# The dt chain ahead of the first gate's function, in a laid order, in a Mamba-2 and differential-attention trunk

## The chip, the core and the metric

The kernel runs on one core of a Trainium2 chip. That core has five engines with an instruction queue each: TensorE (PE in the profile), VectorE (DVE), ScalarE (ACT), GpSimd (POOL) and SyncE (SP), which issues most DMAs. An engine takes the instructions of its queue strictly in order and waits on semaphores for the others. The metric is the device time of one execution in microseconds, lower is better.

## The reference, cut to what matters

The input is a sequence of 512 tokens of 1024 features. Layer A is a Mamba-2 mixer, layer B a differential attention that uses one shared key and value projection of layer A's output.

```python
h = rms_norm(x, norm_g)
zxbcdt = h @ w_in                       # z: 2048, x: 2048, B: 1024, C: 1024, dt: 32
xbc = silu(causal_depthwise_conv(xbc, conv_w, conv_b))
dt = softplus(dt_raw + dt_bias)         # 32 heads
a = -exp(a_log)
y = ssd_chunked_scan(xs * dt, a * dt, bm, cm)
y = y + d_skip * xs
u = y * silu(z)                         # the gate
u = u * rsqrt(mean over 256 features of u*u + eps) * g
x = x + u @ w_out
k, v = shared_kv(x); x = x + diff_attention(x, k, v); return rms_norm(x)
```

The scan treats the 32 heads in eight groups (four heads each, one B and one C of 128 states per group).

## The kernel before, in words

Float32 products are made out of three matmuls each: a matrix is split into a rounded part `hi` and a rest `lo`, and hi·hi, hi·lo and lo·hi are summed in a PSUM bank. Weights arrive in 1 MB segments (two `raw` buffers); ScalarE writes `whi` in four casts per segment and VectorE `wlo` in four subtractions (two buffers each). Tokens are not normalised before the products of layer A: the reciprocal root mean square of each token is put on the results, as `r_col` (one value per token, for results with tokens on partitions) or `r_row` (the same as a row, for results with features on partitions).

The work around the change is the start of layer A:

- **The gate of the first two groups** (`pz0`, four PSUM banks for four times 128 tokens): segments 0 and 1. Before the change `z_out` evicts it on ScalarE, as SiLU of bank times `r_col`, eight instructions of 128x256 (`zs`).
- **The dt chain**: `scales` makes `r_col` from the squared sums of the tokens and, through a matmul of a diagonal (`aps_r`), `r_row`. 32 small matmuls make `ps_dt`; `pre`, `e1`, `q1`, `pl`, `dtp`, `adt` and a scan make the decays `acs`, which go to memory (`acs_d`) and come back spread over the partitions as `dec`, 1 MB per group. GpSimd subtracts and masks `dec`, ScalarE exponentiates it. `tok` is a transposed copy of dtp, acs and toe.
- **Group g** (`group_proj`): two segments into four banks `pg{g}_0..3` (B, C and two halves of x). `conv` works in place on a bank: VectorE multiplies by `r_row`, ScalarE writes `xc` (Identity with a weight and a bias), VectorE adds three shifted products, ScalarE takes SiLU of `xc`. The bank is free again after the last shifted product. Group 0's are xc16, xc24, xc0, xc1, in this order; group 1's are xc17, xc25, xc2, xc3.
- **The scan of group g** (`ssd`): `pbt`, `pcb`, `pxt{g}_0`, `pxt{g}_1` transpose or multiply the xc tiles (pxt0_0 reads xc0, pxt0_1 reads xc1), `xdt`, `dx`, `xe`, `psA`, `psB`, `pyd` follow, then the gating `dx*zs`, its squares, a root, the scaled `tmp` and its transposes `pyt`.

Four PSUM banks carry the tag `mm`: `pz0` holds all four, so `pg0_0` waits until the first of them is evicted, and group 1's banks wait for group 0's convolutions.

The order on each engine is made at build time by a list scheduler with its own idea of costs. The wrappers `V`, `A` and `T` pin instructions to the order in which they are written while their `on` is set. `fetch`, called from `use`, lays the casts of a segment two segments ahead of the products, at high priority. A ScalarE function that is not in the loaded table set costs an `ACT_TABLE_LOAD`; the loads stand in the built program.

Of the kernel before, what the change touches and what calls it, by code (L numbers as in the profile page):

```python
# [25 lines left out]
H = 32  # L26
# [12 lines left out]
C_GA, C_GK, C_GB, C_GG, C_SG, C_DTB, C_AL, C_CB, C_CW = 0, 8, 16, 24, 40, 41, 42, 43, 75  # L39
# [24 lines left out]
def trunk(ctx, tc, x, x_t, par, w_dt, w_in, w_out, w_kvqg, w_bo, d_skip, lam_qk, fin_g, out):  # L64
    nc = tc.nc
    V, A, T = (Ordered(tc, e) for e in (nc.vector, nc.scalar, nc.tensor))
    GP = nc.gpsimd

    const = ctx.enter_context(tc.tile_pool(name="const", bufs=1))
    res = ctx.enter_context(tc.tile_pool(name="res", bufs=1))  # L70
    wp = ctx.enter_context(tc.tile_pool(name="wp", bufs=2))
    small = ctx.enter_context(tc.tile_pool(name="small", bufs=2))
# [13 lines left out]
    def long_bank(name):  # L86
        return psum.tile([P, 512], F32, tag="long", name=name)
# [10 lines left out]
    prm = const.tile([P, C_CB], F32, name="prm")  # L98
# [3 lines left out]
    ident = const.tile([P, P], F32, name="ident")  # L102
# [18 lines left out]
    ready = {}  # L121
# [166 lines left out]
    def run(gen):  # L288
        for _ in gen:
            pass  # L290
# [18 lines left out]
            sq = small.tile([P, D], F32, tag="wide", name=f"sq{t}", bufs=2)  # L309
        A.activation(sq, x_tok[:, t, :], AF.Square, accum_out=ss[:, t:t + 1])  # L310

    def scales(tag, ss):

        V.tensor_scalar(out=ss, in0=ss, scalar1=ROOT2 / D, scalar2=ROOT2 * EPS, op0=ALU.mult, op1=ALU.add)
        col = const.tile([P, NT], F32, tag="r_col", name=f"{tag}r_col")
        V.tensor_copy(col, rsqrt(ss, NT, "y"))
        w = small.tile([P, NT + 1, P], F32, tag="wide", name=f"{tag}diag", bufs=2)
        GP.memset(w[:, NT], 1.0)
        for t in range(NT):
            GP.tensor_tensor(out=w[:, t], in0=ident, in1=col[:, t:t + 1].to_broadcast([P, P]), op=ALU.mult)  # L320
        ps = long_bank(f"{tag}ps_r")
        T.on = True
        T.matmul(ps, lhsT=w[:, NT], rhs=w[:, 0:NT].rearrange("p t n -> p (t n)"), start=True, stop=True)
        T.on = False
        row = res.tile([P, S], F32, tag="r_row", name=f"{tag}r_row")
        A.copy(row, ps)
        return col, row
# [18 lines left out]
    def tok_mm(ps, t, b, w):  # L346
        tk = slice(t * P, (t + 1) * P)
        for k in range(4):
            kk = 4 * b + k
            mm3(ps, (hh[:, kk, tk], hl[:, kk, tk]), (w[0][:, k, :], w[1][:, k, :]), b == 0 and k == 0, b == 1 and k == 3)  # L350
            yield
# [10 lines left out]
    zt = {}  # L362
# [22 lines left out]
    begin = small.tile([P, 1], F32, name="begin", bufs=1)  # L385
# [14 lines left out]
    for k in range(4, KD):  # L400
        split_x(k)
    fetch(2)
    for t in range(NT):
        nc.sync.dma_start(x_tok[:, t, :], x[t * P:(t + 1) * P, :])
    ss = sm.tile([P, NT], F32, name="ass")
    for t in range(NT):
        squares(ss, t)
    r_col, r_row = scales("a", ss)
    V.tensor_scalar(out=sg1, in0=prm[:, C_SG:C_SG + 1], scalar1=0.5 * (1.0 - LAM0), scalar2=None, op0=ALU.mult)
    dtw_raw = sm.tile([P, KD, H], F32, name="dtw_raw")  # L410
    nc.sync.dma_start(dtw_raw[:], w_dt)

    V.tensor_tensor(out=dtw_raw, in0=dtw_raw, in1=prm[:, C_GA:C_GA + KD].unsqueeze(2).to_broadcast([P, KD, H]), op=ALU.mult)
    ps_dt = ss_bank("ps_dt")
    T.on = True
    for k in range(KD):
        for c in range(NQ):  # L420
            T.matmul(ps_dt[c * H:(c + 1) * H, 0:P], lhsT=dtw_raw[:, k, :], rhs=xt[k // 2][:, k % 2, c * P:(c + 1) * P],
                     start=k == 0, stop=k == KD - 1)
    T.on = False
    pre = sm.tile([P, P], F32, name="pre")
    for c in range(NQ):
        sl = slice(c * H, (c + 1) * H)
# [2 lines left out]
    e1 = sm.tile([P, P], F32, name="e1")  # L429
    A.activation(e1, pre, AF.Abs)  # L430
    A.activation(e1, e1, AF.Exp, scale=-1.0)

    q1 = sm.tile([P, P], F32, name="q1")
    V.tensor_scalar(out=q1, in0=e1, scalar1=2.0, scalar2=None, op0=ALU.add)
# [8 lines left out]
    V.scalar_tensor_tensor(out=pl, in0=pl, scalar=2.0, in1=q1, op0=ALU.add, op1=ALU.mult)  # L443
    dtp = sm.tile([P, P], F32, name="dtp")
    V.scalar_tensor_tensor(out=dtp, in0=pre, scalar=0.0, in1=pl, op0=ALU.max, op1=ALU.add)
    ea = sm.tile([P, 1], F32, name="ea")
    A.activation(ea, prm[:, C_AL:C_AL + 1], AF.Exp)
    adt = sm.tile([P, P], F32, name="adt")
    V.tensor_scalar(out=adt, in0=dtp, scalar1=ea, scalar2=-1.0, op0=ALU.mult, op1=ALU.mult)
    ones = sm.tile([P, P], F32, name="ones")  # L450
# [3 lines left out]
    acs_d = tc.dram_tile([H, NQ, P], F32, name="acs_d")  # L454
    for c in range(NQ):
        nc.sync.dma_start(acs_d[:, c, :], acs[c * H:(c + 1) * H, :])
    toe = sm.tile([P, P], F32, name="toe")
    A.activation(toe, acs, AF.Exp, scale=-1.0, bias=acs[:, P - 1:P])
    dsk = const.tile([P, H], F32, name="dsk")
    nc.sync.dma_start(dsk[:], d_skip.partition_broadcast(P))  # L460


    w0 = use(("z", 0, 1))
    for t in range(NT):
        run(tok_mm(pz0[t], t, 1, w0))
        z_out(0, t, pz0[t])


    ps_tt = ss_bank("ps_tt")
    for i, src in enumerate((dtp, acs, toe)):  # L470
        T.transpose(ps_tt[:, i * P:(i + 1) * P], src, ident)
    tok = const.tile([P, 4, NQ, H], F32, name="tok")
    V.tensor_copy(tok[:, 0:3].rearrange("p a c h -> p (a c h)"), ps_tt[:, 0:3 * P])
    A.activation(tok[:, 3], tok[:, 1], AF.Exp)
    dt_tok, acs_tok, toe_tok, eacs_tok = (tok[:, i] for i in range(4))


    def z_proj(j):
        pz = [mm_bank(f"pz{j}_{t}") for t in range(NT)]
        for b in range(2):  # L480
            w = use(("z", j, b))
            for t in range(NT):
                yield from tok_mm(pz[t], t, b, w)
                if b:
                    z_out(j, t, pz[t])

    def conv(ps, ft, name, bufs):
        xc = bp2.tile([P, S], F32, tag=f"xc_{name}", name=f"xc{ft}", bufs=bufs)
        at = C_CW - C_CB + 4 * ft
        cw = [prc[:, at + k:at + k + 1] for k in range(4)]  # L490

        u = ps
        V.tensor_tensor(out=u, in0=ps, in1=r_row, op=ALU.mult)
        A.activation(xc, u, AF.Identity, scale=cw[3], bias=prc[:, ft:ft + 1])
        for k in (2, 1, 0):
            d = 3 - k
            V.scalar_tensor_tensor(out=xc[:, d:], in0=u[:, :S - d], scalar=cw[k], in1=xc[:, d:], op0=ALU.mult, op1=ALU.add)
        A.activation(xc, xc, AF.Silu)
        return xc

    def group_proj(g):
        pg = [mm_bank(f"pg{g}_{i}") for i in range(4)]
        fts = [(16 + g, "b", 1), (24 + g, "c", 2), (2 * g, "x0", 1), (2 * g + 1, "x1", 1)]
        outs = []
        for b in range(2):
            wh, wl = use(("g", g, b))
            for i in range(4):
                cs = slice(i * P, (i + 1) * P)
                for k in range(4):
                    kk = 4 * b + k  # L510
                    mm3(pg[i], (wh[:, k, cs], wl[:, k, cs]), (hh[:, kk, :], hl[:, kk, :]),
                        b == 0 and k == 0, b == 1 and k == 3)
                    yield
# [34 lines left out]
    def decays(gs):  # L548

        for g in gs:  # L550
            hs = slice(R * g, R * g + R)
            both = bp.tile([P, N_DEC], F32, tag="dec", name=f"dec{g}", bufs=2)
            dec = both[:, 0:R * NQ * P].rearrange("p (h c l) -> p h c l", h=R, c=NQ)
            een = both[:, R * NQ * P:].rearrange("p (h q) -> p h q", h=R)
            nc.sync.dma_start(both[:, 0:R * NQ * P],
                                acs_d[hs].rearrange("h c l -> (h c l)").partition_broadcast(P))
            GP.tensor_copy(een, dec[:, :, 1:3, P - 1])
            for h in range(R):
                GP.tensor_tensor(out=dec[:, h], in0=dec[:, h], in1=acs_tok[:, :, R * g + h].unsqueeze(2).to_broadcast([P, NQ, P]), op=ALU.subtract)
                GP.affine_select(out=dec[:, h], in_=dec[:, h], compare_op=ALU.is_ge, fill=-BIG, base=0,  # L560
                                 pattern=[[0, NQ], [1, P]], channel_multiplier=-1)
            decs[g] = (dec, een, both)

        for g in gs:
            A.activation(decs[g][2], decs[g][2], AF.Exp)

    def ssd(g):
        bc, cc, x0, x1 = conv_out.pop(g)
# [516 lines left out]
    y, f, o, dst = half(3, 0)  # L1085
# [77 lines left out]
```

## Time and profile before

| | us |
|---|---|
| median of three runs | 709.59 (709.17 to 709.61) |
| the profiled execution's own time | 709.26 |
| its span, first to last instruction | 707.5 |
| PE busy | 697.5 (99%) |
| DVE, ACT, POOL busy | 519.5, 430.1, 111.7 |
| granted TensorE clock | 0.999 |

Busy time of PE says that it nearly always had work; where it had none is read from its waits and from the starts of its matmuls, which in a full stream of 128x512 follow each other at 0.227 us although each row is shown with 0.39 us.

### The profile page before, as it was taken

How to read it: one execution, taken by the hardware profiler on the slowest of the kernel's cores; microseconds unless marked ns; L12 is line 12 of the kernel's file. 1: busy time of each engine (PE TensorE's matmuls, PEld its weight loads, DVE VectorE, ACT ScalarE, POOL GpSimd, SP SyncE). 2: the span in 40 equal slices, each digit the busy share in tenths (PEclk: the TensorE clock that was granted, in tenths of full speed). 3: DMA queues.
4: the chain of work that ended last, by engine and by line, in shares of the span. 5: the costliest groups of instructions: out<-in, count | busy, mean ns of one | idle time of the engine just before them, and what ended most of it. 6: DMA issues, size and time to landing. Idle time of an engine off the chain costs nothing.

```text
span 707.5 us, 10916 instructions
## 1 busy us (share of the span) xinstructions
PE 697.5 (99%) x4030; PEld 590.8 (84%) x4030; DVE 519.5 (73%) x1197; ACT 430.1 (61%) x955; POOL 111.7 (16%) x158
## 2 busy tenths in 40 slices
PE   9999999999999999999999999999999999999996
PEld 7777888888888888888888879888988998899885
DVE  5479964889579569568997856566767757785886
ACT  6739672764744537538535367676667766756556
POOL 0009421503306024050110101000000000000002
PEclk9999999999999999999999999999999999999999
DMA  8644313333133331331221311412211221122003
GB/s 303 246 151 152 120 59 127 113 120 120 60 119 120 120 120 60 119 120 59 73 100 68 120 60 36 152 60 93 87 61 60 75 105 59 61 101 80 31 0 120
DMA packets 13493, 70.88 MB, mean 100 GB/s; under 512 B 1792, under 2 KB 3328, under 8 KB 6016
## 3 DMA queue, kind: packets, MB, share of 16 engines
q1 hardware_dynamic: 13008, 69.90, 27.6%
q8 instruction: 32, 0.52, 0.3%
q10 hardware_dynamic: 432, 0.28, 0.1%
q14 instruction: 21, 0.17, 0.1%
HBM read 68.02 MB, written 2.16 MB: 99 GB/s over the span
## 4 chain that ended last, share of the span: by engine, by line
PE 88%; ACT 4%; DVE 3%; DMA 3%; issue 1%; SPq 0%; ACTq 0%; DVEq 0%
PE pg L55 20%; PE po L55 16%; PE pz L55 9%; PE pt L55 7%; PE pv L55 6%; PE pq L55 6%; PE pk L55 6%; PE pb L55 3%; DMA raw<-in_w_in 3%; PE sc L55 3%; PE pyd L55 2%; PE pc L55 2%; ACT whi L55 1%; PE pxt L55 1%; PE psA L55 1%; PE pyt L55 1%
## 5 line engine op out<-in xcount | busy, mean ns | idle before, releaser
L55 DVE SCALAR_TENSOR_TENSOR wlo<-raw,prm,whi 128x512 fp32r<-128x512 f32 (+1 forms) x256 | 150.8, 637 | 56.1 <-ACT whi L55 55.6
L55 ACT ACTIVATE whi<-raw,prm 128x512 fp32r<-128x512 f32 (+1 forms) x256 | 136.8, 607 | 62.8 <-issue 13.1
L55 PE MATMUL pg<-a_hi,whi 128*128 128x512 f32 x256 | 102.2, 399 | 0.4 <-ACT zs L55 0.3
L55 PE MATMUL pg<-a_lo,whi 128*128 128x512 f32 x256 | 101.1, 395 | 0.0
L55 PE MATMUL pg<-a_hi,wlo 128*128 128x512 f32 x256 | 100.0, 396 | 0.0
L55 DVE SCALAR_TENSOR_TENSOR xc<-pg,prc,xc 128x511 f32<-128x511 f32 (+2 forms) x96 | 69.9, 739 | 7.5 <-ACT xc L55 7.1
L55 PEld LDWEIGHTS pg<-a_hi,whi 128*128 128x128 f32 x256 | 48.1, 188 | 10.5 <-ACT zs L55 0.6
L55 PEld LDWEIGHTS pg<-a_hi,wlo 128*128 128x128 f32 x256 | 48.1, 188 | 9.8
L55 PEld LDWEIGHTS pg<-a_lo,whi 128*128 128x128 f32 x256 | 48.1, 188 | 9.6
L55 PE MATMUL po<-whi,yh 128*128 128x512 f32 x128 | 50.8, 397 | 0.4 <-ACT yh L55 0.4
L55 PE MATMUL po<-wlo,yh 128*128 128x512 f32 x128 | 50.8, 397 | 0.0
L55 PE MATMUL po<-whi,yl 128*128 128x512 f32 x128 | 50.1, 395 | 0.0
L55 PE MATMUL pz<-wlo,a_hi 128*128 128x512 f32 x128 | 49.3, 394 | 0.0
L55 PE MATMUL pz<-whi,a_hi 128*128 128x512 f32 x128 | 48.9, 396 | 0.0
L55 PE MATMUL pz<-whi,a_lo 128*128 128x512 f32 x128 | 48.8, 390 | 0.0
L968 POOL TENSOR_TENSOR ot<-x_tok,fg 128x512 f32<-128x512 f32 x4 | 5.0, 1290 | 246.4 <-DVE x_tok L55 246.4
L55 ACT ACTIVATE s<-s,mx 128x128 f32<-128x128 f32 (+3 forms) x64 | 35.5, 556 | 9.7 <-DVE mx L55 9.3
L55 ACT ACTIVATE xc<-pg,prc 128x512 f32<-128x512 f32 x32 | 24.8, 776 | 24.5 <-DVE pg L55 19.6
L595 POOL TENSOR_TENSOR xe<-xdt,tok 128x256 f32<-128x256 f32 x24 | 14.1, 614 | 161.5 <-DVE xdt L55 161.5
L55 DVE CUSTOM_DVE_ANT_0 s<-sc,bias 128x128 f32<-128x128 f32 (+3 forms) x64 | 29.3, 487 | 12.3 <-PE sc L55 11.8
L55 PE MATMUL pv<-whi,b_hi 128*128 128x256 f32 x128 | 36.9, 289 | 0.0
L55 PE MATMUL pv<-whi,b_lo 128*128 128x256 f32 x128 | 36.2, 283 | 0.0
(238 smaller groups left out, 1676.5 us busy)
## 6 DMA issues: line engine op xcount, KB each, us to landing
raw<-in_w_in SPq DMA_DIRECT2D x22, 1024.0 KB, 4.9
raw<-in_w_kvqg SPq DMA_DIRECT2D x16, 1024.0 KB, 4.8
dec<-acs_d SPq DMA_DIRECT2D x8, 1024.0 KB, 4.8
raw<-in_w_out SPq DMA_DIRECT2D x8, 1024.0 KB, 4.7
raw<-in_w_bo SPq DMA_DIRECT2D x4, 1024.0 KB, 4.7
x_tok<-in_x SPq DMA_DIRECT2D x4, 512.0 KB, 9.0
out<-ot SPq DMA_DIRECT2D x6, 256.0 KB, 2.3
raw<-in_w_in SPq DMA_DIRECT2D x4, 256.0 KB, 4.7
```

What stands on the lines that cost most here:

```text
L55: i = op(*args, **kw)
L595: GP.tensor_tensor(out=xe[:, c], in0=xdt[:, c], in1=toe_tok[:, c, hs].unsqueeze(2).to_broadcast([P, R, HD]), op=ALU.mult)
L968: GP.tensor_tensor(out=o, in0=y, in1=f, op=ALU.mult)
```

## The change

- The gate's eight SiLUs on the banks become eight `tensor_scalar` on VectorE (`z_raw`: bank times `r_col`), three banks' worth right behind `r_col`, the fourth behind the copy of `r_row`. SiLU is then taken in place on `zs` by ScalarE, queued behind the last convolution function of group 0 (`issue_after(conv_end)`).
- The gate's second half of products stands ahead of the dt chain in the program, and the casts of segments 2 and 3 are laid by hand: segment 2 behind the first three banks, segment 3 behind the scan. VectorE and ScalarE are pinned over the whole chain.
- A one-element `Exp` is put behind the copy of `r_row`; `ea` moves behind the first Exp of the chain; `tok[:, 3]` (an Exp) moves to where the decays are exponentiated.
- The loads of `dtw_raw` and `dsk` are written ahead of segments 2 and 3.

```diff
+    w0 = ready.pop(("z", 0, 1))
     for t in range(NT):
         nc.sync.dma_start(x_tok[:, t, :], x[t * P:(t + 1) * P, :])
+    dtw_raw = sm.tile([P, KD, H], F32, name="dtw_raw")
+    nc.sync.dma_start(dtw_raw[:], w_dt)
+    nc.sync.dma_start(dsk[:], d_skip.partition_broadcast(P))
+    splits = {n: load(n) for n in (2, 3)}
...
-    r_col, r_row = scales("a", ss)
+    for t in range(NT):
+        run(tok_mm(pz0[t], t, 1, w0))
+    V.on = True
+    r_col, diag = scale_cols(ss)
+
+    def z_raw(t):
+        for i in range(2):
+            zt[i, t] = bp2.tile([P, 256], F32, tag="zs", name=f"zs0_{t}_{i}", bufs=12)
+            V.tensor_scalar(out=zt[i, t], in0=pz0[t][:, i * 256:(i + 1) * 256], scalar1=r_col[:, t:t + 1], scalar2=None, op0=ALU.mult)
+
+    for t in range(3):
+        z_raw(t)
+    A.on = True
+    for piece in splits[2]():
+        lay(piece)
...
+    A.copy(r_row, ps_r)
+    A.activation(begin, ident[:, 0:1], AF.Exp)
+    z_raw(3)
...
+    A.activation(ea, prm[:, C_AL:C_AL + 1], AF.Exp)
...
         nc.sync.dma_start(acs_d[:, c, :], acs[c * H:(c + 1) * H, :])
+    for piece in splits[3]():
+        lay(piece)
     A.activation(toe, acs, AF.Exp, scale=-1.0, bias=acs[:, P - 1:P])
-    w0 = use(("z", 0, 1))
-    for t in range(NT):
-        run(tok_mm(pz0[t], t, 1, w0))
-        z_out(0, t, pz0[t])
+    A.on = V.on = False
...
-        A.activation(xc, xc, AF.Silu)
+        conv_end[0] = A.activation(xc, xc, AF.Silu)
...
+        if g == 0:
+            with tc.issue_after(conv_end[0].ins):
+                for t in range(NT):
+                    for i in range(2):
+                        A.activation(zt[i, t], zt[i, t], AF.Silu)
...
+        if gs[0] == 0:
+            A.activation(tok[:, 3], tok[:, 1], AF.Exp)
```

What the scheduler makes of it on ScalarE, from the load ahead of group 0's first SiLU to its last, before the change (numbers behind the names tell buffers apart; xc16, xc24, xc0 and xc1 are group 0's tiles, whi5 is segment 5, dec0 and dec1 are the decays of groups 0 and 1):

```order
L55 ACT_TABLE_LOAD
L55 ACTIVATE xc16_570<-xc16_570 128x512
L55 ACTIVATE xc0_608<-pg0_2_484,prc_72 128x512
L55 ACTIVATE whi5_548<-raw5_546,prm_70 128x512 x4
L55 ACTIVATE xc24_589<-xc24_589 128x512
L55 ACTIVATE xc1_627<-pg0_3_485,prc_72 128x512
L55 ACT_TABLE_LOAD
L55 ACTIVATE dec0_442<-dec0_442 128x2056
L55 COPY bt0_662<-pbt0_658 128x384
L55 ACT_TABLE_LOAD
L55 ACTIVATE xc0_608<-xc0_608 128x512
L55 ACTIVATE xc1_627<-xc1_627 128x512
```

The same stretch with the change, from segment 5 on (ahead of these rows stand the Identities of xc16, xc24 and xc0, a table load and the SiLU of xc16; behind them the eight SiLUs of `zs`):

```order
L55 ACTIVATE whi5_549<-raw5_547,prm_70 128x512 x4
L55 ACT_TABLE_LOAD
L55 ACTIVATE dec0_442<-dec0_442 128x2056
L55 ACTIVATE xc1_628<-pg0_3_486,prc_72 128x512
L55 ACT_TABLE_LOAD
L55 ACTIVATE xc24_590<-xc24_590 128x512
L55 COPY bt0_671<-pbt0_667 128x384
L55 ACTIVATE xc0_609<-xc0_609 128x512
L55 ACT_TABLE_LOAD
L55 ACTIVATE dec1_461<-dec1_461 128x2056
L55 ACT_TABLE_LOAD
L55 ACTIVATE xc1_628<-xc1_628 128x512
```

The SiLU of xc24 and the Identity of xc1 stand behind dec0 now, and the SiLU of xc1 behind dec1 and two more table loads.

On PE, where group 0's two x tiles are transposed among group 1's products (pg1), before the change:

```order
L55 MATMUL pxt0_0_666<-ident_74,xc0_608 128x128 x4
L55 MATMUL pg1_2_636<-a_hi_80,wlo4_489 128x512
L55 MATMUL pg1_2_636<-a_hi_80,whi4_488 128x512
L55 MATMUL pg1_2_636<-a_lo_81,whi4_488 128x512
L55 MATMUL pg1_2_636<-a_hi_80,wlo4_489 128x512
L55 MATMUL pg1_3_637<-a_hi_80,whi4_488 128x512
L55 MATMUL pg1_3_637<-a_lo_81,whi4_488 128x512
L55 MATMUL pg1_3_637<-a_hi_80,wlo4_489 128x512
L55 MATMUL pg1_3_637<-a_hi_80,whi4_488 128x512
L55 MATMUL pxt0_1_673<-ident_74,xc1_627 128x128 x4
```

With the change, from the product of xc24 and xc16 on:

```order
L55 MATMUL pcb0_662<-xc24_590,xc16_571 128x128 x4
L55 MATMUL pxt0_0_675<-ident_74,xc0_609 128x128 x4
L55 MATMUL pg1_2_645<-a_hi_80,whi4_489 128x512
L55 MATMUL pg1_2_645<-a_lo_81,whi4_489 128x512
L55 MATMUL pg1_2_645<-a_hi_80,wlo4_490 128x512
L55 MATMUL pg1_2_645<-a_hi_80,whi4_489 128x512
L55 MATMUL pg1_2_645<-a_lo_81,whi4_489 128x512
L55 MATMUL pg1_2_645<-a_hi_80,wlo4_490 128x512
L55 MATMUL pxt0_1_682<-ident_74,xc1_628 128x128 x4
```

Between the two transpositions stand six products now, where eight stood; ahead of pxt0_1 stand 51 products of group 1, where 47 stood.

On ScalarE, at the end of layer A, group 7's squares (`tmp7,ss47<-dx7`), the casts of segment 32 and the scaled rows (`tmp7<-dx7`), before the change:

```order
L55 COPY hst7_3377<-psA7_3378 128x256
L55 ACTIVATE tmp7_3389,ss47_3388<-dx7_3354 128x256 x4
L55 ACTIVATE whi32_3740<-raw32_3738,prm_70 128x256 x8
L55 ACTIVATE tmp7_3389<-dx7_3354,y_y_3446 128x256 x2
L55 CAST yh7_3462<-pyt7_0_3464 128x256
```

With the change:

```order
L55 COPY hst7_3386<-psA7_3387 128x256
L55 ACTIVATE tmp7_3398,ss47_3397<-dx7_3363 128x256 x3
L55 ACTIVATE whi32_3749<-raw32_3747,prm_70 128x256 x4
L55 ACTIVATE tmp7_3398,ss47_3397<-dx7_3363 128x256
L55 ACTIVATE whi32_3749<-raw32_3747,prm_70 128x256 x4
L55 ACTIVATE tmp7_3398<-dx7_3363,y_y_3455 128x256 x2
L55 CAST yh7_3471<-pyt7_0_3473 128x256
```

The last of the four squares stands behind four of the eight casts now.

More of the change, by code (lines that the diff above doesn't have):

```diff
@@ L310, in squares, with scale_cols @@
         A.activation(sq, x_tok[:, t, :], AF.Square, accum_out=ss[:, t:t + 1])
-    def scales(tag, ss):
+    def scale_cols(ss):
         V.tensor_scalar(out=ss, in0=ss, scalar1=ROOT2 / D, scalar2=ROOT2 * EPS, op0=ALU.mult, op1=ALU.add)
-        col = const.tile([P, NT], F32, tag="r_col", name=f"{tag}r_col")
+        col = const.tile([P, NT], F32, tag="r_col", name="ar_col")
         V.tensor_copy(col, rsqrt(ss, NT, "y"))
-        w = small.tile([P, NT + 1, P], F32, tag="wide", name=f"{tag}diag", bufs=2)
+        w = small.tile([P, NT + 1, P], F32, tag="wide", name="adiag", bufs=2)
         GP.memset(w[:, NT], 1.0)
@@ L320, in scales @@
             GP.tensor_tensor(out=w[:, t], in0=ident, in1=col[:, t:t + 1].to_broadcast([P, P]), op=ALU.mult)
[L321 to L327, printed above, removed]
+        return col, w
     def turn_rows(tag, t, xn, hh, hl):
@@ L402, in trunk @@
     fetch(2)
+    w0 = ready.pop(("z", 0, 1))
     for t in range(NT):
         nc.sync.dma_start(x_tok[:, t, :], x[t * P:(t + 1) * P, :])
+    dtw_raw = sm.tile([P, KD, H], F32, name="dtw_raw")
+    nc.sync.dma_start(dtw_raw[:], w_dt)
+    dsk = const.tile([P, H], F32, name="dsk")
+    nc.sync.dma_start(dsk[:], d_skip.partition_broadcast(P))
+    splits = {n: load(n) for n in (2, 3)}
     ss = sm.tile([P, NT], F32, name="ass")
@@ L407, in trunk @@
         squares(ss, t)
-    r_col, r_row = scales("a", ss)
+    for t in range(NT):
+        run(tok_mm(pz0[t], t, 1, w0))
     V.tensor_scalar(out=sg1, in0=prm[:, C_SG:C_SG + 1], scalar1=0.5 * (1.0 - LAM0), scalar2=None, op0=ALU.mult)
-    dtw_raw = sm.tile([P, KD, H], F32, name="dtw_raw")
-    nc.sync.dma_start(dtw_raw[:], w_dt)
+    V.on = True
     V.tensor_tensor(out=dtw_raw, in0=dtw_raw, in1=prm[:, C_GA:C_GA + KD].unsqueeze(2).to_broadcast([P, KD, H]), op=ALU.mult)
+    r_col, diag = scale_cols(ss)
[8 more added lines that the diff above has]
+        lay(piece)
+    ps_r = long_bank("aps_r")
     ps_dt = ss_bank("ps_dt")
     T.on = True
+    T.matmul(ps_r, lhsT=diag[:, NT], rhs=diag[:, 0:NT].rearrange("p t n -> p (t n)"), start=True, stop=True)
     for k in range(KD):
@@ L423, in trunk @@
     T.on = False
+    r_row = res.tile([P, S], F32, tag="r_row", name="ar_row")
+    A.copy(r_row, ps_r)
+    A.activation(begin, ident[:, 0:1], AF.Exp)
+    z_raw(3)
     pre = sm.tile([P, P], F32, name="pre")
@@ L431, in trunk @@
     A.activation(e1, e1, AF.Exp, scale=-1.0)
+    ea = sm.tile([P, 1], F32, name="ea")
+    A.activation(ea, prm[:, C_AL:C_AL + 1], AF.Exp)
     q1 = sm.tile([P, P], F32, name="q1")
@@ L445, in trunk @@
     V.scalar_tensor_tensor(out=dtp, in0=pre, scalar=0.0, in1=pl, op0=ALU.max, op1=ALU.add)
-    ea = sm.tile([P, 1], F32, name="ea")
-    A.activation(ea, prm[:, C_AL:C_AL + 1], AF.Exp)
     adt = sm.tile([P, P], F32, name="adt")
@@ L456, in trunk @@
         nc.sync.dma_start(acs_d[:, c, :], acs[c * H:(c + 1) * H, :])
+    for piece in splits[3]():
+        lay(piece)
     toe = sm.tile([P, P], F32, name="toe")
     A.activation(toe, acs, AF.Exp, scale=-1.0, bias=acs[:, P - 1:P])
-    dsk = const.tile([P, H], F32, name="dsk")
-    nc.sync.dma_start(dsk[:], d_skip.partition_broadcast(P))
-    w0 = use(("z", 0, 1))
-    for t in range(NT):
-        run(tok_mm(pz0[t], t, 1, w0))
-        z_out(0, t, pz0[t])
+    A.on = V.on = False
     ps_tt = ss_bank("ps_tt")
@@ L473, in trunk @@
     V.tensor_copy(tok[:, 0:3].rearrange("p a c h -> p (a c h)"), ps_tt[:, 0:3 * P])
-    A.activation(tok[:, 3], tok[:, 1], AF.Exp)
     dt_tok, acs_tok, toe_tok, eacs_tok = (tok[:, i] for i in range(4))
@@ L485, in z_proj @@
                     z_out(j, t, pz[t])
+    conv_end = [None]
     def conv(ps, ft, name, bufs):
```

## The prediction

> **What bounds the kernel now.** First the page of the profile: busy times and the chain that ended last.
>
> ```profile
> PE 697.5 (99%) x4030; PEld 590.8 (84%) x4030; DVE 519.5 (73%) x1197; ACT 430.1 (61%) x955; POOL 111.7 (16%) x158
> PE 88%; ACT 4%; DVE 3%; DMA 3%; issue 1%; SPq 0%; ACTq 0%; DVEq 0%
> ```
>
> TensorE sets the time; the change removes no matmul, so it can move only what PE waits. The waits of PE, second view, are few:
>
> ```profile
> PE pxt L55 <- ACT xc L55: 1.4, 1, 1.4
> PE po L55 <- ACT yh L55: 0.4, 1, 0.4
> PE pg L55 <- ACT zs L55: 0.3, 1, 0.3
> ```
>
> Third, PE's timeline there, since a row drawn with 0.39 us hides a short wait (columns: start, us, engine, line, operation, tiles):
>
> ```profile
> 30.56 0.50 PE L55 MATMUL pg<-a_hi,whi 128*128 128x512 f32 x1 [0.32 <-ACT zs L55]
> 44.68 0.40 PE L55 MATMUL pg<-a_lo,whi 128*128 128x512 f32 x1
> 45.13 0.33 PE L55 MATMUL ps_tt<-ident,acs 128*128 128x128 f32 x1
> ...
> 52.24 0.39 PE L55 MATMUL pg<-a_hi,wlo 128*128 128x512 f32 x1
> ...
> 52.92 0.39 PE L55 MATMUL pg<-a_hi,wlo 128*128 128x512 f32 x1
> 53.41 0.47 PE L55 MATMUL pg<-a_hi,whi 128*128 128x512 f32 x1
> ...
> 63.38 0.39 PE L55 MATMUL pg<-a_lo,whi 128*128 128x512 f32 x1
> 65.17 0.44 PE L55 MATMUL pxt<-ident,xc 128*128 128x128 f32 x2 [1.40 <-ACT xc L55]
> ```
>
> From 52.24 to 52.92 PE starts three products, so one takes 0.68 / 3 = 0.227 us from start to start. So 45.13 is 0.22 late (it waits for `acs`) and 53.41 is 0.26 late (group 1's first bank). With 0.32 and 1.40 that is **2.2 us in reach** of the change. All else is loss.
>
> **The change, part by part.** *The gate on VectorE.* A `tensor_scalar` of 128x256 out of PSUM isn't in the trace; nearest is the sum of 128x256 with one operand in PSUM, 0.41 with the next start 0.33 behind.
>
> ```profile
> 24.49 0.17 DVE L55 COPY ar_col<-y_y 128x4 f32<-128x4 f32 x1
> 26.55 2.74 DVE L55 SCALAR_TENSOR_TENSOR wlo<-raw,prm,whi 128x512 fp32r<-128x512 f32 x4 [1.90 <-ACT whi L55]
> 53.84 0.69 DVE L55 TENSOR_TENSOR pg<-pg,ar_row 128x512 f32<-128x512 f32 x1
> 54.43 2.28 DVE L55 SCALAR_TENSOR_TENSOR xc<-pg,prc,xc 128x510 f32<-128x510 f32 x3
> 76.67 0.41 DVE L55 TENSOR_TENSOR hst<-psA,hst 128x256 f32<-128x256 f32 x1
> 77.00 0.74 DVE L55 SCALAR_TENSOR_TENSOR xc<-pg,prc,xc 128x511 f32<-128x511 f32 x1
> ```
>
> Six cost 2.0 to 2.5, of which VectorE's 1.90 idle covers nearly all: `wlo` of segment 2 starts at 27.0 at worst and PE wants it behind `aps_r` and `ps_dt`, near 30.7. Without that cover it would cost at most 0.5. The first bank is free by 25.5, so the 0.32 goes. The three banks are no longer behind a table load and casts on ScalarE.
>
> *The dt chain.* `pre` needs `ps_dt` (ends near 30.9); before it stood behind segment 3's subtractions. The scan ends near 39 in place of 45, so the 0.22 goes, and `acs_d` and the 1 MB decays leave 6 us sooner:
>
> ```profile
> 48.02 0.81 SPq L555 DMA_DIRECT2D dec<-acs_d  x2
> 52.86 0.20 POOL L557 COPY dec<-dec 128x8 f32<-128x8 f32 x1 [26.57 <-DMA dec<-acs_d]
> 65.55 2.39 POOL L560 TENSOR_SCALAR_AFFINE_SELECT dec<-dec 128x512 f32<-128x512 f32 x4
> raw<-in_w_in SPq DMA_DIRECT2D x5, 1024.0 KB, 8.8
> ```
>
> GpSimd thus ends both decays near 62, not 67.94. Segment 5's load now stands behind those DMAs on SP: issued near 43, landed near 52 by the median of 8.8; ScalarE casts it at 54.3 below, so it costs nothing, and 1 us for each us that it lands later.
>
> *Group 0's convolutions.* They follow PE now, not the subtractions: group 0's second half starts at 30.56 - 0.32 + 48 x 0.227 = 41.1. Bank 2 (xc0) is complete 38 products and three transpositions (0.35) later, 50.3 with the last row's tail. VectorE has bank 1 at 48.3, does 0.60 and three shifted products (2.1 by the row of three), and ends bank 2's multiply at 51.6. The first bank is free near 52.3, PE there at 52.4: the 0.26 goes.
>
> *ScalarE's queue, the term that decides.* Prices by starts:
>
> ```profile
> 54.63 0.63 ACT L55 ACTIVATE xc<-xc 128x512 f32<-128x512 f32 x1
> 55.17 0.76 ACT L55 ACTIVATE xc<-pg,prc 128x512 f32<-128x512 f32 x1
> 55.83 2.55 ACT L55 ACTIVATE whi<-raw,prm 128x512 fp32r<-128x512 f32 x4
> ...
> 58.81 0.76 ACT L55 ACTIVATE xc<-pg,prc 128x512 f32<-128x512 f32 x1
> 59.59 1.28 ACT L55 ACT_TABLE_LOAD   x1
> 60.88 1.93 ACT L55 ACTIVATE dec<-dec 128x2056 f32<-128x2056 f32 x1
> 62.71 0.46 ACT L55 COPY bt<-pbt 128x384 f32<-128x384 f32 x1
> 63.19 1.28 ACT L55 ACT_TABLE_LOAD   x1
> 64.48 1.15 ACT L55 ACTIVATE xc<-xc 128x512 f32<-128x512 f32 x2
> 65.65 1.28 ACT L55 ACT_TABLE_LOAD   x1
> ```
>
> From 51.6 ScalarE does, in its new order: Identity 0.78, load 1.29, SiLU 0.54, casts 2.57, load 1.29, dec0 1.83, Identity 0.78, load 1.29, SiLU 0.54, bt 0.40, SiLU 0.63, load 1.29, dec1 1.95, load 1.29, SiLU of xc1 0.63: 17.1, so **xc1 is there at 68.7**. Neither decay is waited for (dec1 is wanted at 64.9). PE: from 53.41 to 63.61 it did 39 products and two groups of transpositions and `pcb`, 10.2 us, of which 39 x 0.227 = 8.85 are products; so the others cost 1.35. From 50.1 to pxt0_1 it now has 61 products, these 1.35 and pxt0_0's 0.5: 15.7, so **PE stands at pxt0_1 at 65.9 and waits 2.8**. Bounds: 2.3 (products as slow as 0.23, each cast and function at its shortest) and 3.3. pcb (63.1) and pxt0_0 (64) just miss their own waits: xc24 is done at 62.6, xc0 at 63.5.
>
> [...]
>
> *Behind it.* The eight SiLUs in place (2.6 to 3.2 us, some 0.32 to 0.40 each, half of a 128x512's work) end near 71.5; the Identity of xc17 follows, and VectorE's queue has xc17's first shifted product ahead of xdt0_1, so it stands until 72.1. Its work from there to the last gating (12 shifted products, 8 subtractions of casts, three multiplies and group 0's and 1's scan parts at the prices above) is 23 to 24.5 us, to about 96.3; then square 0.6, load, dec2, load, two `zs` of gate 1, four `tmp`:
>
> ```profile
> 67.52 0.60 PE L55 MATMUL pxt<-ident,xc 128*128 128x128 f32 x4
> 101.47 1.04 PE L55 MATMUL pyt<-ident,tmp 128*128 128x128 f32 x8
> 98.87 1.70 ACT L55 ACTIVATE tmp<-dx,y_y 128x256 f32<-128x256 f32 x4
> ...
> 401.16 3.31 ACT L55 ACTIVATE whi<-raw,prm 128x256 fp32r<-128x256 f32 x8 [0.44 <-ACT tmp L55]
> 404.37 0.90 ACT L55 ACTIVATE tmp<-dx,y_y 128x256 f32<-128x256 f32 x2
> 407.30 0.50 PE L55 MATMUL po<-whi,yh 128*128 128x512 f32 x1 [0.35 <-ACT yh L55]
> ```
>
> That is 7.4 more, 103.7 to 104.3. PE went from pxt0_1 to pyt0 in 33.95 and has one product more on that way, so it is there at 68.7 + 34.2 = 102.9 and ends pyt0 0.5 late. I take **0.5**, bounds 0 and 1.5. At the end of layer A the fourth square stands behind four casts, so it ends near 403.4 where it ended at 400.7; the root and the scaled rows follow it 1.2 later than now, and some of that is slack: **0.5**, bounds 0 and 1.0.
>
> **Sum:** -0.32 - 0.22 - 0.26 - 1.40 + 2.8 + 0.5 + 0.5 = +1.6. On the profiled execution's own 709.26 (span 707.5 and 1.76 around it) that is **710.9**; that execution is 0.33 under the median of 709.59. Bounds: -2.2 + 2.3 = +0.1 and -1.9 + 3.3 + 1.5 + 1.0 = +3.9, so 709.4 to 713.2. What a measurement can tell from no change is 0.2%, 1.4 us: under 708.2 or over 711.0.
>
> **Rivals.** *B, the earlier chain pays:* if ScalarE has xc1 before PE asks, the four waits just go: 709.26 - 2.2 = 707.1. For it: dt chain, decays and GpSimd run 6 us sooner, and the built order has 21 table loads where the profile has 23:
>
> ```profile
> L55 ACT ACT_TABLE_LOAD x23 | 29.5, 1283 | 7.9 <-DVE xc L55 5.5 <-PEq L1156 1.2 <-DVE y_i L55 0.9
> ```
>
> Against it: ScalarE's start is set by bank 2, which PE completes only at 50.3, and two table loads and dec1 now stand between two SiLUs that ran as one row at 64.48. [...]
>
> *C, slower, from the gate's functions:* the eight SiLUs and xc17's Identity stop VectorE for about 5 us (67.5 to 72.1); if VectorE then needs over 25.5 us to the last gating, because GpSimd's work on dec2 slows its subtractions, each us more is a us at pyt0 (from about 96.0 on): 2 more there, and the tail at its upper bound, 713.2. For it: VectorE is 73% busy, and a sum of subtractions and products beside GpSimd may be short. Against it: that sum is made of rows in which GpSimd worked too (54.43 to 77.00, beside 65.55).
>
> *D, nothing new decides:* the first wait at its lower bound and no other: 709.26 + 0.1 = 709.4. The laid order then does what it says, the chain is early, but only trades one wait for another.
>
> **How the numbers follow.** A 0.55, B 0.14, C 0.18, D 0.13. A's own range 709.4 to 713.0 straddles 711.0 about evenly. Faster: B and a little of D, 0.16. Same: half of A and most of D, 0.41. Slower: half of A and C, 0.43. The range 708.2 to 713.0 leaves out B and the end of C.
>
> **What would show it.** PE's waits name pxt <- ACT xc near 66 to 69 with 2.3 to 3.3; no wait at pg <- zs; the scan near 39; ACT's loads 21. B shows as no wait at pxt; C as pyt waiting over 1.5 near 103. Wrong would be I if xc1's SiLU starts before 66, or if a stall stands where I see none, above all at segment 5's cast (near 54) or in groups 2 to 6, whose order also moved by a few rows and which I cost at nothing.

## The result

The changed kernel takes 715.53 us (median of five runs, 714.93 to 716.51) where the kernel before takes 709.59 (708.92 to 710.65): a ratio of 1.0087, with an interval of 1.0075 to 1.0098. It is 5.9 us slower. The prediction said 710.9 us, 708.2 to 713.0, with 0.43 on slower: the direction holds, the size is some four times too small. One execution of the kernel before (4014.71 us) and one of a run below (3683.86 us) lie far outside all others and are left out of the ratios.

The page of the changed kernel, busy times and the chain that ended last:

```profile
PE 700.3 (98%) x4030; PEld 591.3 (83%) x4030; DVE 526.4 (74%) x1205; ACT 427.5 (60%) x954; POOL 114.2 (16%) x158
PE 83%; DVE 6%; ACT 5%; issue 3%; DMA 2%; POOL 1%; ACTq 0%; POOLq 0%; SPq 0%
```

TensorE does the same 4030 products, and the span grew by 6.3 us (707.5 to 713.8). Its share of the chain fell from 88% to 83%. What it waited for, in the view of waits (total, times, longest):

```profile
PE pxt L55 <- ACT xc L55: 2.8, 1, 2.8
PE warm L55 <- POOL ident masks.py:199: 1.5, 1, 1.5
PE po L55 <- DVE x_tok L55: 0.9, 1, 0.9
PE pcb L55 <- ACT xc L55: 0.7, 1, 0.7
PE pyt L55 <- DVE yl L55: 0.6, 1, 0.6
PE po L55 <- ACT yh L55: 0.4, 1, 0.4
```

The wait for `zs` is gone, the wait for xc has doubled, and three waits are new: `x_tok`, `pcb`, `yl`. They add up to less than 6.3, so a second reading is needed. Since both programs issue the same products, there are points up to which the same ones are done in both; there the starts can be set beside each other (from the two timelines of TensorE):

| product at that point | before, us | after, us | difference |
|---|---|---|---|
| group 0's products behind the dt matmuls | 31.14 | 30.37 | -0.8 |
| first product of group 1 | 53.41 | 52.27 | -1.1 |
| behind pxt0_1, clock just full again | 71.40 | 73.27 | +1.9 |
| behind pyt0 | 103.83 | 106.59 | +2.8 |
| group 3's products, behind pcb of group 2 | 152.34 | 156.33 | +4.0 |
| group 6's products | 306.88 | 311.12 | +4.2 |
| behind pyd of group 6 | 350.62 | 355.77 | +5.2 |
| tail of layer A, second pyt | 408.34 | 414.51 | +6.2 |

Behind that the difference stays (6.3 over the whole span): layer B costs the same. So the loss has four places: 3.0 us at pxt0_1, 0.9 up to pyt0, 2.4 in groups 2 to 6, 1.0 in the tail of layer A. ScalarE ahead of pxt0_1, and TensorE there (timelines; start, us, engine, line, operation):

```profile
62.80 0.63 ACT L55 ACTIVATE xc<-xc 128x512 f32<-128x512 f32 x1
63.45 1.28 ACT L55 ACT_TABLE_LOAD   x1
64.74 1.92 ACT L55 ACTIVATE dec<-dec 128x2056 f32<-128x2056 f32 x1
66.69 1.28 ACT L55 ACT_TABLE_LOAD   x1
67.98 0.63 ACT L55 ACTIVATE xc<-xc 128x512 f32<-128x512 f32 x1
```

```profile
65.45 0.40 PE L55 MATMUL pg<-a_hi,wlo 128*128 128x512 f32 x1
68.66 0.79 PE L55 MATMUL pxt<-ident,xc 128*128 128x128 f32 x4 [2.82 <-ACT xc L55]
69.10 0.78 PE L55 MATMUL pg<-a_hi,whi 128*128 128x512 f32 x1
...
70.10 0.63 PE L55 MATMUL pg<-a_hi,wlo 128*128 128x512 f32 x1
70.53 0.63 PE L55 MATMUL pg<-a_hi,whi 128*128 128x512 f32 x1
...
73.04 0.39 PE L55 MATMUL pg<-a_lo,whi 128*128 128x512 f32 x1
73.27 0.39 PE L55 MATMUL pg<-a_hi,wlo 128*128 128x512 f32 x1
```

The start of pxt0_1 is 2.98 later than it would be in a full stream (68.66 - 65.45 is 3.21, of which 0.23 is the product itself). Behind it the products start 0.43 apart (70.10 to 70.53) in place of 0.23. The windows of the changed kernel say why. A row gives a stretch, its length, the busy time of PE, PEld, DVE, ACT and POOL, then the granted clock of TensorE and two columns for DMA:

```profile
66.00:69.00 3.00, 0.34 (x3) 0.34 (x4) 1.79 (x3) 2.97 (x5) 0.00 (x0) 1.00 0.00 0
69.10:72.40 3.30, 3.30 (x11) 2.63 (x9) 0.64 (x1) 2.62 (x8) 0.00 (x0) 0.50 0.00 0
72.50:76.00 3.50, 3.50 (x17) 2.87 (x17) 3.02 (x6) 1.17 (x2) 1.76 (x3) 1.00 0.00 0
```

For 3.3 us behind the wait the clock stands at 0.50, which costs half of that at this place, 1.7 us, and is in no view of waits: TensorE counts as busy for all of the 3.30.

### The profile page after: what moved, and what is told of

Read it like the earlier page. It is cut to its first block, busy times and chain, and to the rows that moved or that the text cites. A ratio compares the mean times of both kernels' runs of the same rounds, so it can differ in the third digit from the quotient of the medians.

```text
span 713.8 us, 10925 instructions
## 1 busy us (share of the span) xinstructions
PE 700.3 (98%) x4030; PEld 591.3 (83%) x4030; DVE 526.4 (74%) x1205; ACT 427.5 (60%) x954; POOL 114.2 (16%) x158
## 4 chain that ended last, share of the span: by engine, by line
PE 83%; DVE 6%; ACT 5%; issue 3%; DMA 2%; POOL 1%; ACTq 0%; POOLq 0%; SPq 0%
PE pg L55 18%; PE po L55 13%; PE pz L55 10%; PE pt L55 7%; PE pv L55 6%; PE pq L55 6%; PE pk L55 6%; PE pb L55 3%; PE sc L55 3%; PE pc L55 2%; PE pyd L55 2%; DVE wlo L55 2%; DMA dec<-acs_d 1%; ACT L55 1%; DVE dx L55 1%
## 5 line engine op out<-in xcount | busy, mean ns | idle before, releaser
L55 DVE SCALAR_TENSOR_TENSOR xc<-pg,prc,xc 128x509 f32<-128x509 f32 (+2 forms) x96 | 70.0, 742 | 11.4 <-ACT xc L55 10.5
L55 ACT ACTIVATE tmp<-dx 128x256 f32<-128x256 f32 x32 | 13.1, 411 | 43.2 <-DVE dx L55 43.2
```

Source lines behind the costliest of these rows:

```text
L55: i = op(*args, **kw)
```

## Experiments

Two theories stood against each other after this reading. **Lateness:** xc1 comes late, VectorE stops behind it, and the new waits further down are the same delay handed on. **Order:** the scheduler, which laid dec1 ahead of xc1's SiLU, also laid groups 1 to 7 in another order (the built ScalarE queue differs from the one before down to the tail of layer A), and that order has waits of its own. A third question was whether the half clock belongs to the length of the wait.

### One function moved: dec1 behind group 0's SiLUs

```diff
-                        A.activation(zt[i, t], zt[i, t], AF.Silu)
+                        last = A.activation(zt[i, t], zt[i, t], AF.Silu)
+            with tc.issue_after(last.ins):
+                A.activation(decs[1][2], decs[1][2], AF.Exp)
...
         for g in gs:
-            A.activation(decs[g][2], decs[g][2], AF.Exp)
+            if g != 1:
+                A.activation(decs[g][2], decs[g][2], AF.Exp)
```

> The changed kernel with one function moved: the Exp of group 1's decays (dec1) stands behind group 0's last SiLU and the eight SiLUs of the gate, so xc1's SiLU follows xc0's and needs no table load of its own. Theory A (the stall at pxt0_1 is the cause, with the half clock behind it, and what stands later than before at 106 and 147 us comes from VectorE's stop in it): xc1 is there at 64, TensorE asks at 65.9, the 2.98 and the 1.6 of half clock go, and with them most of the 0.9 by 106.6 and the 1.0 at 147.5: 715.5 - 4.6 - 1.9 = 709.0. Theory B (the later waits come from the order of the later groups, which moved by itself): only 4.6 goes, 710.9. Theory C (xc1's place is not the cause): over 714.

Measured: 708.35 us, ratio 0.9985 (0.9976 to 0.9994). One function in another place turns a loss of 5.9 into a gain of 1.0; theory A had 709.0, theory B 710.9. TensorE's waits now:

```profile
PE warm L55 <- POOL ident masks.py:199: 1.5, 1, 1.5
PE po L55 <- ACT yh L55: 0.4, 1, 0.4
PE po L55 <- DVE hst L55: 0.2, 1, 0.2
PE pyt L55 <- ACT tmp L55: 0.2, 1, 0.2
```

pxt0_1 starts at 65.07 with no wait, and the waits for `x_tok`, `pcb` and `yl` are gone too. So dec1's place is the cause of nearly all. But moving it gave the scheduler another order as well: from 113 us on this build is, on every engine, row for row that of the kernel before, while the changed kernel differs from it down to the tail of layer A. So this run can't tell lateness from order.

### A late xc1 in an unchanged order

The scheduler doesn't count table loads. One-element functions of other sets between xc0's and xc1's SiLU therefore delay xc1 and leave every other instruction of every engine where it stands in the kernel just shown. Exp alone (`hid2`), Exp and Sqrt (`hid3`) and Exp, SiLU, Exp (`hid4`) cost two, three and four loads of 1.28 us each in the traces (the diff shows `hid3`):

```diff
-        conv_end[0] = A.activation(xc, xc, AF.Silu)
+        if ft == 1:
+            with tc.issue_after(conv_end[0].ins):
+                mark = A.activation(begin, ident[:, 0:1], AF.Exp)
+                mark = A.activation(begin, ident[:, 0:1], AF.Sqrt)
+            with tc.issue_after(mark.ins):
+                conv_end[0] = A.activation(xc, xc, AF.Silu)
+        else:
+            conv_end[0] = A.activation(xc, xc, AF.Silu)
```

> The kernel e1_dec1_late with one one-element Exp between the SiLU of xc0 and that of xc1. It costs ScalarE two table loads, which the scheduler does not count, so every other instruction keeps its place. xc1 is there 2.8 us later (1.28 + 0.2 + 1.28), near 66.6, TensorE asks at 65.07: a gap of 1.5. No half clock behind it under any theory (1.56 in the kernel before and 2.26 in dose4 had none): 708.35 + 1.5 = 709.9. Lag theory (a late xc1 makes the later groups late too, in the same order): 0.5 to 1 on top.

> The same with a one-element Exp and a one-element Sqrt, three loads: xc1 4.25 us later, a gap of 3.0 on TensorE at the place and of the length that the changed kernel has, but with the order of all later work as in e1_dec1_late. Gate theory (the granted clock halves behind a gap of about 3 us): products 0.43 apart for some 3 us, 3.0 + 1.6 = 4.6 more, 713.0; without it 711.4. Lag theory (the waits at 147, 356 and 414 us in the changed kernel come from the lateness): these waits are here too, 2 to 2.7 more, 715 to 715.6. Order theory (they come from the changed order of the later groups): they are not here.

> The same with Exp, SiLU, Exp on one element, four loads: xc1 5.5 us later, a gap of 4.3. Gate theory: half clock again for about 3 us, 708.35 + 4.3 + 1.6 = 714.3, by the lag theory 716 to 717. If the half clock lasts the longer the longer the gap, over 715 by the order theory as well.

| | gap at pxt0_1, us | time, us | above the kernel without it | ratio to the kernel before |
|---|---|---|---|---|
| no extra function | none | 708.35 | | 0.9985 |
| hid2 | 1.73 | 710.97 | 2.6 | 1.0022 (1.0013 to 1.0031) |
| hid3 | 3.24 | 712.96 | 4.6 | 1.0050 (1.0038 to 1.0063) |
| hid4 | 4.76 | 714.98 | 6.6 | 1.0080 (1.0064 to 1.0095) |

The waits of `hid3` and the windows around its half clock:

```profile
PE pxt L55 <- ACT xc L55: 3.1, 1, 3.1
PE warm L55 <- POOL ident masks.py:199: 1.5, 1, 1.5
PE po L55 <- ACT yh L55: 0.4, 1, 0.4
```

```profile
66.00:67.80 1.80, 0.00 (x0) 0.00 (x0) 1.80 (x4) 1.77 (x3) 0.00 (x0) 1.00 0.00 0
67.80:74.60 6.80, 5.67 (x16) 4.61 (x17) 1.74 (x3) 6.76 (x13) 1.76 (x3) 0.50 0.00 0
74.60:76.00 1.40, 1.40 (x8) 1.15 (x7) 0.74 (x1) 0.62 (x1) 0.00 (x0) 0.99 0.00 0
```

Behind a gap of 3.24 the clock is 0.50 here as well, and none of the later waits follows it: lateness of xc1 is not handed on to groups 2 to 7. The time, 712.96, is what the gate and the order theory gave together (713.0), but in part by chance. The half clock lasted 6.8 us and not 3; counted from the first products of layer A, TensorE is 5.9 us later behind it than without the added functions, and 0.9 of that comes back by the end of pyt0. `hid4`, with 714.98, is 0.7 above the 714.3 of the order theory; its half clock, too, lasted 6.8 us. `hid2` has a clock of 1.00 in every window from 66 to 76 us and lost 1.1 more than I gave it, in a second wait of 1.4 behind it (`po` on VectorE's `hst`); the other two don't have it, probably because TensorE at half clock asks later, which was not tested.

### The change's order without the late xc1

The counterpart: the changed kernel with group 1's decays put through SiLU in place of Exp. In the trace no table load stands around it (dec1 starts at 64.10, xc1's SiLU at 65.91 in place of 67.98); all else stays in place, row by row.

```diff
-            A.activation(decs[g][2], decs[g][2], AF.Exp)
+            A.activation(decs[g][2], decs[g][2], AF.Silu if g == 1 else AF.Exp)
```

> The changed kernel with group 1's decays put through SiLU in place of Exp (so its output is not the reference's; that is the part left out), which takes away the two table loads around dec1 and leaves every other instruction of every engine in its place. xc1 is there 2.6 us earlier, near 66.1, TensorE asks at 65.9: the wait at pxt0_1 falls from 2.98 to about 0.4 and no half clock follows. Order theory (the waits of 0.9 at 147.5, 1.0 at 355.8 and 0.8 at 414.5 us belong to the order of the later groups): these three stay, 715.5 - 2.6 - 1.6 = 711.3. Lag theory (they come from the late xc1): they go too, 708.6 to 709.3. If the eight SiLUs and xc17 behind them are what stops VectorE, pyt0 still waits 0.3 to 0.6.

Measured: 713.23 us, ratio 1.0052 (1.0037 to 1.0067), with a granted clock of 0.999. The waits:

```profile
PE pyt L55 <- ACT tmp L55: 1.1, 1, 1.1
PE pcb L55 <- ACT xc L55: 0.9, 2, 0.7
PE po L55 <- DVE x_tok L55: 0.9, 1, 0.9
PE pyt L55 <- DVE yl L55: 0.6, 1, 0.6
PE po L55 <- ACT yh L55: 0.4, 1, 0.4
```

The wait at pxt0_1 and the half clock are gone, and the three later waits are there to the last digit: from start to start 0.89, 0.97 and 0.75 us too long, where the changed kernel has 0.90, 0.97 and 0.76. They belong to the order. I had put 711.3 on this outcome. Of the 1.9 above that, 1.05 is pyt0, whose wait grew from 0.55 to 1.6: TensorE now comes earlier, and pyt0 is there no sooner than its own chain allows. Another 0.3 is a wait at pcb of group 6. The chain that ends at pyt0 does not run through VectorE's stop behind xc17. In the changed kernel it runs through a transfer of decays (start, us, what):

```profile
82.25 0.63 POOL hst L626
82.90 4.91 DMA dec<-acs_d
...
96.68 1.72 DVE dx L55 x2
```

Without the late xc1 it takes the same way; GpSimd's timeline shows it:

```profile
79.41 0.62 POOL L626 TENSOR_TENSOR hst<-hst,dec 128x256 f32<-128x256 f32 x1 [2.01 <-DVE hst L55]
85.31 0.81 POOL L571 COPY dec<-dec 128x8 f32<-128x8 f32 x1 [5.29 <-DMA dec<-acs_d]
86.21 4.46 POOL L573 TENSOR_TENSOR dec<-dec,tok 128x512 f32<-128x512 f32 x4
90.63 0.73 POOL L660 TENSOR_TENSOR dx<-dx,tmp 128x256 f32<-128x256 f32 x1
91.33 1.99 POOL L574 TENSOR_SCALAR_AFFINE_SELECT dec<-dec 128x512 f32<-128x512 f32 x3
93.28 1.43 POOL L660 TENSOR_TENSOR dx<-dx,tmp 128x256 f32<-128x256 f32 x2
```

The second `hst` reads the tail of dec0's buffer; dec2's 1 MB goes into that buffer behind it; GpSimd's additions to `dx`, on which the last gating waits, stand among dec2's subtractions and masks. In the order before, the first of the three additions stands ahead of dec2:

```profile
80.99 0.85 POOL L644 TENSOR_TENSOR dx<-dx,tmp 128x256 f32<-128x256 f32 x1 [3.21 <-DVE tmp L55]
82.74 0.19 POOL L557 COPY dec<-dec 128x8 f32<-128x8 f32 x1 [0.90 <-DMA dec<-acs_d]
```

### The eviction alone

The kernel before with only the gate's eviction on VectorE and SiLU in place behind group 0's convolutions; dt chain, casts and decays as they were.

```diff
-        z_out(0, t, pz0[t])
+        for i in range(2):
+            zt[i, t] = bp2.tile([P, 256], F32, tag="zs", name=f"zs0_{t}_{i}", bufs=12)
+            V.tensor_scalar(out=zt[i, t], in0=pz0[t][:, i * 256:(i + 1) * 256], scalar1=r_col[:, t:t + 1], scalar2=None, op0=ALU.mult)
...
-        A.activation(xc, xc, AF.Silu)
+        conv_end[0] = A.activation(xc, xc, AF.Silu)
...
+        if g == 0:
+            with tc.issue_after(conv_end[0].ins):
+                for t in range(NT):
+                    for i in range(2):
+                        A.activation(zt[i, t], zt[i, t], AF.Silu)
```

> The kernel before with one part of the change: VectorE evicts the first gate's banks times r_col, and SiLU is taken in place behind group 0's last convolution function; the dt chain, the casts and the decays stay where they were written. Theory A (what makes the change slow is the decays' place among group 0's SiLUs, which comes with the early chain): order of xc0, xc1 and the decays as before, so the wait at pxt0_0 stays near 1.4 and the waits at 30.56 (0.32) and at the transposition of acs (0.22) go: 709.3 - 0.5 = 708.8, between 708.3 and 709.5. Theory B (the eight SiLUs at 65 to 68 us are what hurts, since the casts of segment 6 and xc17 stand behind them): 2.6 later for dec1 and the casts, a wait of 1 to 2 among group 1's products, 710 to 711.5.

Measured: 706.86 us, ratio 0.9963 (0.9951 to 0.9975): 2.5 us faster than the kernel before, faster than either kernel and than any other run. I had expected the 1.4 at pxt0_0 to stay. It went, because ScalarE, without the eight evictions and their table load ahead of `r_row`, runs some 3 us earlier:

```profile
58.12 1.93 ACT L55 ACTIVATE dec<-dec 128x2056 f32<-128x2056 f32 x1
60.07 1.28 ACT L55 ACT_TABLE_LOAD   x1
61.36 0.63 ACT L55 ACTIVATE xc<-xc 128x512 f32<-128x512 f32 x1
62.17 0.64 ACT L55 ACTIVATE xc<-xc 128x512 f32<-128x512 f32 x1 [0.18 <-DVE xc L55]
62.72 2.55 ACT L55 ACTIVATE zs<-zs 128x256 f32<-128x256 f32 x8
```

xc0's SiLU starts at 61.36 in place of 64.48. The scan, too, is early without any laid order: `acs` starts at 41.52, where it stood at 44.65 before and at 39.10 with the whole change. GpSimd's order is the same as before, row by row, and no wait is left between the start of the span and the tail of layer A (the view of waits has 1.5 for `warm`, 0.4 for `pz` on `a_hi` and 0.4 for `po` on `yh`). The 2.5 us are a little more than the 2.2 that the prediction called in reach, and this part alone has them; the laid order adds nothing to it in these runs.

### Redundant copies: a dose that moved

To lengthen the wait of the kernel before I put redundant in-place copies of xc0 ahead of its SiLU, two and four of them:

```diff
+        if ft == 0:
+            for _ in range(2):
+                A.activation(xc, xc, AF.Copy)
         A.activation(xc, xc, AF.Silu)
```

> The kernel before with two redundant in-place copies of xc0 ahead of its SiLU (some 0.54 us each on ScalarE), which lengthen the wait at pxt0_0 from 1.4 to about 2.5. Theory A (TensorE's granted clock falls to a half for some 3 us after an idle time of this length): 1.1 of wait and up to 1.6 of half clock, 709.6 + 2.7 = 712.3, with matmuls 0.43 apart behind the wait. Theory B (the half clock in the changed kernel does not come from the length of the wait): 1.1 alone, 710.7, matmuls 0.227 apart.

> The kernel before with four such copies: the wait at pxt0_0 becomes about 3.6. Theory A: 2.2 of wait and 1.6 of half clock, 713.4. Theory B: 711.8. If the price of the half clock grows with the wait (2 us or more of it), 713.8 or over.

Measured: 708.30 us (0.9986, 0.9977 to 0.9995) with two, 717.28 us (1.0108, 1.0095 to 1.0121) with four. Neither expectation holds, and as a dose both fail: the scheduler counts a copy, and moved the transpositions. With two it laid both behind more of group 1's products, and the kernel got faster by doing more, for the wait of 1.4 was a matter of where TensorE asks. With four nearly every group was laid anew:

```profile
PE pxt L55 <- ACT xc L55: 2.1, 1, 2.1
PE po L55 <- DVE x_tok L55: 1.5, 2, 1.2
...
PE aps_r L55 <- POOL adiag L320: 1.0, 1, 1.0
PE pz L55 <- DVE xc L55: 0.8, 1, 0.8
```

Only one thing is to be had from it: its gap of 2.26 us at pxt (from start to start) leaves the clock at 1.00.

### The tail of layer A

The changed kernel with the casts of segment 32 behind group 7's fourth square; on ScalarE one square moves, nothing elsewhere.

```diff
-                    lay(piece)
+                    with tc.issue_after(sq_end[0].ins):
+                        lay(piece)
...
+    sq_end = [None]
...
-            A.activation(tm[:, c], u[:, c], AF.Square, accum_out=ss4[:, c:c + 1])
+            sq_end[0] = A.activation(tm[:, c], u[:, c], AF.Square, accum_out=ss4[:, c:c + 1])
```

> The changed kernel with the eight casts of segment 32 behind group 7's fourth square on ScalarE, as in the kernel before; nothing else moves on any engine. If the square behind four casts is the whole of the wait of 0.76 at 414.5 us (the prediction put 0.5 on it, bounds 0 and 1.0), that wait goes and the time falls by 0.8, to 714.7; the wait of 0.6 at 412.7, which the kernel before has too, stays. If something else makes it late, no change, 715.5.

In the trace the wait `PE pyt <- DVE yl` is gone and TensorE gains 1.0 us against the changed kernel between the products at 357 and at 414 us; the wait ahead of it stays, which the view of waits gives as 0.4 (`po` on `yh`; 0.6 is the time from start to start). The median, 715.15 us (ratio 1.0072, 1.0046 to 1.0097), is 0.4 lower, which the intervals can't tell from 0.8 or from nothing. So the mechanism is shown by the trace, the gain not by the times.

## Why the prediction was wrong

**What held.** The three waits ahead of group 1 did go: 0.8 us by the first product of group 1, where the sum had 0.32 + 0.22 + 0.26 (the table's -1.1 has 0.3 from the start of the span, ahead of the change). The scan came at 39.10 ("near 39"). ScalarE has 21 loads. xc1 was there at 68.6 ("68.7"), TensorE stood at pxt0_1 at 65.7 ("65.9") and waited 2.82 ("2.8"). Segment 5's load, issued at 43.43 in place of 35.38, landed at 52.30, ahead of its cast at 54.14, and cost nothing. So the term that was to decide was right as a duration.

**The first step that failed is the price of that wait.** The sum counts it at its own length. In the trace 3.3 us at half clock stood behind it, 1.7 us more at this place. The rows of the kernel before could not show this, since the longest wait there, 1.56 from start to start, has a clock of 1.00 behind it, but a bound for it would have been in place: what TensorE does when it comes back was taken for granted. In the time of a whole execution this step is the smaller one. By the estimate from their granted clocks (last section) two of the five executions of the changed kernel had no such stretch, and they took 715.49 and 714.93 us, hardly less than the median of 715.53. Without the late xc1, where TensorE comes earlier, the wait at pyt0 grew from 0.55 to 1.6; that it did so in these two as well is an estimate.

**The second step is the sentence on "groups 2 to 6, whose order also moved by a few rows and which I cost at nothing".** It is the larger one. Three runs split the loss: 708.35 with dec1 behind, 713.23 with the change's order but without its late xc1, 715.53 as it is. So by difference 4.9 us are the order that the scheduler made for groups 1 to 7 once dec1 stood ahead of xc1's SiLU, and 2.3 are the late xc1 with its half clock, less than the 2.98 + 1.7 it costs at the spot, mostly because pyt0 would have waited anyway. In that order stand 0.9 at pcb of group 2, 0.97 at `x_tok`, 0.76 in the tail, and up to 1.6 at pyt0. Which rows make the first two was not tested. The traces give a place for each. The chain that ends at pcb of group 2 leaves TensorE at 124.7 in the changed kernel and goes through a transfer of decays, GpSimd, the gating and ScalarE; in the kernel before it is TensorE alone. Ahead of `x_tok` VectorE stands still for 2.48 us up to 340.35, at `yl`, which waits for ScalarE's `yh`, and then has no break longer than 0.3 up to `x_tok` at 355.04; in the order before, four subtractions of casts and a multiply stand ahead of that `yl`, and it is not waited for.

**pyt0:** forecast 0.5 with bounds 0 and 1.5, found about 0.6 at the spot and 0.9 to the next common product; but the mechanism was wrong, and that the size came out is luck. The prediction led the path through VectorE's stop behind xc17. The stop came as forecast (VectorE starts again at 71.76, "72.1"), but the chain runs through dec2's transfer and GpSimd, and the last gating ended at 98.4 in place of 96.3; TensorE, at half clock for a while, was there at 104.5 in place of 102.9, so that two errors nearly cancelled.

**Tail:** forecast 0.5 with bounds 0 and 1.0, found 0.76. Mechanism right, shown by the move of one square.

**The base of the sum.** It adds to the profiled execution's 709.26; on the median of 709.59 the same sum gives 711.2, which changes nothing above.

**Rivals.** B, the earlier chain pays, gave 707.1 if xc1 is there before TensorE asks; the eviction alone does just this, 706.86. What I held against B (ScalarE's start is set by bank 2, two loads stand between two SiLUs) is true of this build and not of the idea: one Exp behind the SiLUs and the same change is 1.0 faster. C looked for a larger wait at pyt0 and no clock; what it takes for granted, that GpSimd's work on decays slows the subtractions, is in the trace of the kernel before: two took 2.50 us at 60.17, beside GpSimd's work on the decays, and four took 2.74 at 26.55, where GpSimd stands still. D expected one wait to take the place of another. None had the order of later groups as a cost.

**Table loads.** The sum took 1.29 us for each, and that is what the changed kernel has: the function starts 1.29 behind the start of the load (63.45 to 64.74, 66.69 to 67.98). What decided is where two of them stand: around dec1's Exp, between two SiLUs.

## What to carry to other kernels

A list scheduler that doesn't know a cost (here the table load, 1.28 us) can lay one function in the wrong place, and the place of that one function can lay everything behind it anew: cost an order that moved far from the change at more than nothing, or pin it, and try the parts of a change apart before giving it up. A wait of the engine that bounds the kernel can cost more than its length: at the transposition of xc0 or xc1 a clock of 0.50 stood behind the four gaps of 2.98 to 4.76 us, and 1.00 behind the three of 1.56 to 2.26. What of it reaches the time depends on whether a later wait takes it in: of the 2.98 and the 1.7 that the changed kernel lost there, 2.3 did, by the difference to the run without the late xc1. To test whether a delay is handed on, delay by something the scheduler doesn't count, so that the order stays.

## What the runs showed of the hardware

The granted clock of TensorE, read in windows of 0.1 us, one trace for each kernel:

| kernel | gap, start to start less one product, us | half clock from, to, us | length |
|---|---|---|---|
| before | 1.56 | none | |
| hid2 | 1.73 | none | |
| dose4 | 2.26 | none | |
| changed | 2.98 | 69.1 to 72.4 | 3.4 |
| after_tail | 3.00 | 69.8 to 73.2 | 3.4 |
| hid3 | 3.24 | 67.8 to 74.6 | 6.8 |
| hid4 | 4.76 | 68.4 to 75.2 | 6.8 |

The lengths are one or two times 3.4 us, not in proportion to the gap. In two kernels the clock falls 0.4 to 0.5 us after TensorE has started again (changed, after_tail), in two while it still waits (at 67.8 with the next start at 68.93 in hid3, at 68.4 with it at 70.75 in hid4). Gaps of 2.98 us and more had a half clock, 2.26 and less had none; no run has a gap between these two, and what sets the clock was not shown.

The half clock is not in every execution of these kernels. The traces of the kernel before and of the changed kernel have a clock of 0.50 at the end of the span as well, from 705.6 to 707.5 and from 710.8 to 713.8 us. From these lengths an estimate: over some 714 us the mean granted clock is 0.998 to 0.999 with the end alone, and 0.995 to 0.996 with a stretch of 3.4 us more. The five executions of the changed kernel have 0.995, 0.996, 0.996, 0.998 and 0.999, so by this estimate the last two had no such stretch. The same holds for one execution of after_tail (0.998, 713.63 us) and one of hid3 (0.999, 712.68 us). These four are 0.0 to 1.5 us under the medians of their kernels. In the other direction, one of twelve executions of the kernel before, taken beside after_tail, has 0.992 and took 715.37 us. None of these five left a trace, so it stays open whether their gaps were of another length or fell at another moment.
